# First MLP product in pairs of 512 and 256 columns, bias source in another buffer, another front and tail

## The chip, the cores and the metric
The kernel runs on one core of a Trainium2 chip. Its engines work side by side: TensorE (matmuls, in the profile PE), VectorE (DVE), ScalarE (ACT), GpSimd (POOL) and SyncE (SP), which mainly starts transfers; transfers run on DMA engines. Memory on the chip is SBUF (128 partitions) and PSUM, where matmuls write, in banks of 512 float columns. The metric is the device time of one execution in microseconds; smaller is better.

## The reference, cut to what matters
One layer of a hybrid decoder on 256 tokens of width 2048, in float32:
```
z = rmsnorm(h) @ w_in                      # q, k, v and two convolution parts u
h = h + concat(moba_attention(q, k, v, rel_bias), conformer_conv(u)) @ w_out
h = h + cross_attention(rmsnorm(h), rmsnorm(mem))      # wq, wk, wv, wo
h = h + square(relu(rmsnorm(h) @ w1)) @ w2             # w1: 2048 x 8192, w2: 8192 x 2048
return rmsnorm(h)
```
With 256 tokens and one block of 256, the block attention is causal attention with a bias that depends on the distance alone.

## The kernel before
All weights are cut on the host into 200 chunks of 128 x 2048 floats. One chunk is one *step*: 0 to 15 the convolution inputs, 16 to 23 the values, 24 to 39 queries and keys, 40 to 47 keys and values of the memory tokens, 48 to 63 the output projection, 64 to 71 the cross attention, 72 to 199 the MLP. The MLP runs four quarters of 32 steps: 16 steps of the first product, in four blocks of 512 hidden columns, then 16 of the second.

To keep float32 precision at TensorE's faster float32r form, each operand is split: ScalarE writes a rounded high part (`wh`, `actH`, `sH`), VectorE subtracts to get the low part (`wl`, `actL`, `sL`). A product is then three matmuls (`mm3`, line 104): high with high, high with low, low with high. In the first MLP product the weights are stationary (128 x 128) and 256 token columns of an activation part stream past; in the second the activations are stationary and 512 weight columns stream. So a step of the first product is 48 matmuls of 256 columns, one of the second 24 of 512.

A step's weights are loaded four steps ahead by SP into one of four buffers (`raw`) and split two steps ahead into one of three (`wh`, `wl`): the split for step j+2 waits until TensorE is through with step j-1. The loop at line 916 writes the order on every engine: for step j first the hooks "early", the load, the high split, the hooks "pre" (evacuations stand here), convolution taps on VectorE as filler, the low split, the hooks "late", the matmuls with "mid" hooks between them, and "post". Each engine works through its list in order.

Accumulation uses four PSUM banks in turn (`mm`): a block takes two. `evac_w1` (line 794) empties them by max with 0 and multiplying with the row norm `RB["2"]`, squares twice on ScalarE and subtracts on VectorE. For the first block the norm is not there in time, so it is emptied two steps later (`lag=2`, line 867), at step 78.

`ring` (line 91) is a set of seven buffers for short-lived tiles, taken in turn. The source of the attention bias, `rev` (line 261), is such a tile; ScalarE starts a transfer at step 8 that writes it 128 times to DRAM, and SP loads the bias back at step 20. The squares of the memory tokens for their norm (`Stats.add`, line 204) take ring tiles from step 8 on.

Where a tile stands in SBUF is set by `shifted` (line 176): with `ACT_SHIFT` the moving activation parts start 64 bytes past the weights modulo 512 bytes, in all products; with `S_SHIFT` the second product's stationary parts start at the same place modulo 512 as the weights that stream. In the value projections (steps 16 to 23 and 44 to 47) weights stream past activations, again 64 bytes apart.

At the end `finish` adds each token half's last bank to the sum, squares it on ScalarE with a row sum, takes the root, scales 2048 columns by halves on VectorE and ScalarE, and SP writes four pieces of 512 columns.

Of the kernel before, what the change touches and what calls it, by code (L numbers as in the profile page):

```python
# [9 lines left out]
F32 = mybir.dt.float32  # L10
F32R = mybir.dt.float32r
# [26 lines left out]
AHEAD = 2  # L38
WOUT_ORDER = [(0, 0), (1, 0), (2, 0), (0, 1), (1, 1), (2, 1), (3, 0), (3, 1)]
STEP_US = 5.25  # L40

ROOM = 128
ACT_SHIFT = {"H0": 16, "H1": 16, "H2": 112, "H3": 112, "L0": 16, "L1": 16, "L2": 112, "L3": 112}
S_SHIFT = {"Ha0": 32, "Ha1": 32, "Hc0": 96, "Hc1": 96, "La0": 32, "La1": 32, "Lc0": 96, "Lc1": 96}
MIX_STEP = 16

# [31 lines left out]
def tile_hybrid_block(ctx: ExitStack, tc: tile.TileContext, xT, memT, w, par, rel, gfin, out):  # L78
# [12 lines left out]
    def ring(shape=(P, 512)):  # L91
        return sb.tile(list(shape), F32, tag="ring", name=nm("ring"), bufs=7)
# [34 lines left out]
    nc.sync.dma_start(part[:, 0:CB], par[:, 0:CB])  # L127
    load(0)
    for i in range(4):
        nc.sync.dma_start(hT[0][:, i, :], xT[:, i, :])  # L130
        nc.sync.dma_start(raw[0][:, i * 512:(i + 1) * 512], w[0, :, i * 512:(i + 1) * 512])
    for g in range(1, 4):
        nc.sync.dma_start(hT[g], xT[:, 4 * g:4 * g + 4, :])
# [2 lines left out]
    relt = sb.tile([8, N_BUCKETS], F32, name="relt")  # L136
    nc.sync.dma_start(relt, rel)

    make_identity(nc, ident)
    pool.memset(ones, 1.0)  # L140


    hooks = {}
# [36 lines left out]
    def new_act(g):  # L180
        act_tiles[g] = tuple(shifted(f"act{x}{g}", ACT_SHIFT[f"{x}{g}"]) for x in "HL")

    def split_act(g, src, gain, i):
        hi, lo = act_tiles[g]
        c = col(gain, 4 * g + i)
        act.activation(hi[:, i, :], src[:, i, :], AF.Copy, scale=c)  # L186
        dve.scalar_tensor_tensor(lo[:, i, :], src[:, i, :], c, hi.bitcast(F32)[:, i, :],
                                 op0=OP.mult, op1=OP.subtract)

    def split_act_group(g, src, gain):  # L190
        new_act(g)
        for i in range(4):
            split_act(g, src, gain, i)

    def act_pair(kt):
        hi, lo = act_tiles[kt // 4]
        return hi[:, kt % 4, :], lo[:, kt % 4, :]


    class Stats:  # L200
# [57 lines left out]
    bias = sb.tile([P, 8, T], F32, tag="acc0", name="bias")  # L258

    def make_bias():  # L260
        rev = ring((8, 512))
        pool.memset(rev[:, 0:384], MASK)
        d = 0
        while d < T:
            e = d
            while e + 1 < T and bucket(e + 1) == bucket(d):
                e += 1
            b = bucket(d)
            pool.tensor_copy(rev[:, 255 - e:256 - d], relt[:, b:b + 1].to_broadcast([8, e - d + 1]))
            d = e + 1  # L270
        return rev
# [12 lines left out]
    def weight_stationary(j, banks, kg, acts, kts=4, cols=512, last=None):  # L284
# [9 lines left out]
            units.append(unit)  # L294
        return units

    def act_stationary(j, banks, kg, acts, last, ts=(0, 1), kts=4):
        units = []
        for i in range(kts):
            def unit(i=i):  # L300
                hi, lo = acts(kg * 4 + i)
                for t in ts:
                    s = slice(t * P, (t + 1) * P)
                    c = slice(i * 512, (i + 1) * 512)
                    mm3(banks[t], banks[t].ap, (hi[:, s], lo[:, s]), (wh[j][:, c], wl[j][:, c]),
                        last and i == kts - 1)
            units.append(unit)
        return units
# [17 lines left out]
    RB = {}  # L326

    def split_both(j, g):
        new_act(g)
# [464 lines left out]
    def evac_w1(b, banks):  # L794
        sT[b] = tuple(shifted(f"mix{x}{MIX[b]}", S_SHIFT[x + MIX[b]], f"s{x}{b}") for x in "HL")
        for n in range(2):
# [34 lines left out]
    def acc_square(t, cb):  # L831
        d = acc[t][:, cb * 512:(cb + 1) * 512]
        act.activation(ring(), d, AF.Square, accum_out=ssq[:, 8 * t + cb:8 * t + cb + 1])  # L833

    def finish(t, bk):
# [6 lines left out]
        for i in range(2):  # L842
            c = slice(1536 + i * T, 1536 + (i + 1) * T)
            d = acc[t][:, c]
            dve.tensor_tensor(d, bk.ap[:, i * T:(i + 1) * T], d, op=OP.add)
            act.activation(ring()[:, 0:T], d, AF.Square, accum_out=ssq[:, 8 * t + 3 + i:8 * t + 4 + i])
            pool.tensor_mul(d, d, gb[3][:, i * T:(i + 1) * T])
            dve.scalar_tensor_tensor(part_ if i == 0 else v, ssq[:, 8 * t + 3 + i:8 * t + 4 + i], 1.0 / D, part_,
                                     op0=OP.mult, op1=OP.add)
# [3 lines left out]
        dve.tensor_scalar(a, a, -0.5, 1.5, op0=OP.mult, op1=OP.add)  # L853
        dve.tensor_tensor(r, y, a, op=OP.mult)
        for c in (0, 1, 2, 3):
            d = acc[t][:, c * 512:(c + 1) * 512]
            if c in (1, 3):
                act.activation(d, d, AF.Copy, scale=r)
            else:
                dve.tensor_scalar(d, d, r, None, op0=OP.mult)  # L860
            nc.sync.dma_start(out[rows, c * 512:(c + 1) * 512], d)

    for q in range(4):
        j0 = MLP0 + 32 * q
        for b in range(4):
            block(j0 + 4 * b, 4, weight_stationary, act_pair, lambda bk, b=b: evac_w1(b, bk),
                  lag=2 if q == b == 0 else 0)
        for cb in range(4):
            jc = j0 + 16 + 4 * cb
            if q == 3 and cb == 3:  # L870
                banks = []

                def first(kg, jc=jc):
# [10 lines left out]
                pe_units[jc + 3] = lambda jc=jc: (  # L884
                    act_stationary(jc + 2, banks, 2, s_pair, False, ts=(1,))
                    + act_stationary(jc + 3, banks, 3, s_pair, True, ts=(1,)))
# [67 lines left out]
def weight_chunks(np, w_in, wk, wv, w_out, wq, wo, w1, w2):  # L954
    chunks = []

    def put(cols, rows):
        a = cols[rows]
        chunks.append(a.reshape(-1, P, a.shape[1]).transpose(1, 0, 2).reshape(P, 2048))
# [26 lines left out]
        put(wo[:, b * 512:(b + 1) * 512], slice(None))  # L986
    for q in range(4):
        for b in range(4):
            for g in range(4):
                put(w1[:, q * 2048 + b * 512:q * 2048 + (b + 1) * 512], rows(g))  # L990
# [41 lines left out]
```

## Time and profile before

| | us |
|---|---|
| median of 3 runs | 1175.96 |
| lowest, highest | 1175.51, 1176.62 |
| profiled execution, whole | 1174.24 |
| its span, first to last instruction | 1172.4 |
| PE busy | 1149.8 (98%) |
| DVE busy | 707.8 (60%) |
| ACT busy | 540.9 (46%) |
| POOL busy | 116.6 (10%) |

The profile is of one execution. Matmuls overlap each other in it, so a busy share of TensorE doesn't tell how fast they follow; that is read from a piece of the chain of waits, its time by its count. "x" is a count of instructions, "<-" names what an idle engine waited for, L a line of the kernel. Helpers hide the caller's line: all matmuls have line 101 and all VectorE work line 67, so operations are told apart by their tiles. "PEld" is a weight load, "SPq" and "ACTq" are starts of transfers. The granted clock is a share of TensorE's 2.4 GHz.

### The profile page before, as it was taken

To read this page: it belongs to the slowest core of one execution; us is meant where nothing else is said; L and a number is where in the kernel's file an instruction comes from. 1 tells how busy PE (TensorE), PEld (TensorE's weight loads), DVE (VectorE), ACT (ScalarE), POOL (GpSimd) and SP (SyncE) were. 2 spreads that over 40 slices of the span, in tenths; PEclk is the share of its full clock that TensorE was granted. 3 is DMA by queue.
4 is the path that set the end of the run, shared out by engine and by line. 5 is a ranking of instruction groups with operands and counts; after the bars stand their busy time and mean duration, and the time that the engine had idled before them with its cause. 6 is when DMAs were issued, how large, how long until landed. Compare 5 with 4: busy or idle time off the path is not lost.

```text
span 1172.4 us, 18441 instructions
## 1 busy us (share of the span) xinstructions
PE 1149.8 (98%) x7976; PEld 1073.0 (92%) x7976; DVE 707.8 (60%) x821; ACT 540.9 (46%) x564; POOL 116.6 (10%) x100
## 2 busy tenths in 40 slices
PE   7989999999999999999999999999999999999996
PEld 7988899999999999999889999889999888999885
DVE  6669998787666668555444545454555454445443
ACT  7525444565666456554333444333444333444342
POOL 2453121012003003000000000000000000000112
PEclk9998999999999999999999999999999999999998
DMA  8865654444554535545655544655554655554632
GB/s 340 288 186 180 221 204 169 162 147 177 184 193 168 199 120 180 216 145 192 240 195 200 180 180 175 221 182 199 193 181 150 227 198 182 190 195 153 217 142 72
DMA packets 35000, 221.02 MB, mean 189 GB/s; under 512 B 3816, under 2 KB 6504, under 8 KB 9448
## 3 DMA queue, kind: packets, MB, share of 16 engines
q1 hardware_dynamic: 33888, 218.29, 52.0%
q10 hardware_dynamic: 1032, 1.57, 0.9%
q8 instruction: 62, 1.02, 0.3%
q14 instruction: 18, 0.15, 0.0%
HBM read 216.18 MB, written 3.67 MB: 188 GB/s over the span
## 4 chain that ended last, share of the span: by engine, by line
PE 93%; DMA 4%; ACT 1%; DVE 1%; issue 0%; SPq 0%; ACTq 0%
PE mm L101 87%; PE cv L101 3%; DMA dram_rev<-ring 3%; PE sm L101 2%; DMA raw<-in_w_dram 1%; DVE wl L67 1%; ACT wh L160 0%; PE sm L813 0%; PE sm L499 0%; PE sm L689 0%; DVE small L67 0%; ACT actH L186 0%; ACT L679 0%; ACT ring L679 0%; ACT ring L210 0%
## 5 line engine op out<-in xcount | busy, mean ns | idle before, releaser
L67 DVE TENSOR_TENSOR wl<-raw,wh 128x2048 fp32r<-128x2048 f32 (+1 forms) x205 | 447.1, 2187 | 305.5 <-ACT wh L160 301.1
L160 ACT ACTIVATE wh<-raw 128x2048 fp32r<-128x2048 f32 x195 | 373.5, 1915 | 505.0 <-PE mm L101 462.5
L101 PE MATMUL mm<-actH,wh 128*128 128x256 f32 x1600 | 452.4, 283 | 11.0 <-ACT wh L334 6.3
L101 PE MATMUL mm<-actH,wl 128*128 128x256 f32 x1600 | 449.0, 281 | 1.8 <-DVE wl L67 1.8
L101 PE MATMUL mm<-actL,wh 128*128 128x256 f32 x1600 | 448.4, 280 | 0.0
L101 PEld LDWEIGHTS mm<-actH,wh 128*128 128x128 f32 x1600 | 302.9, 189 | 11.7 <-ACT wh L334 6.5
L101 PEld LDWEIGHTS mm<-actH,wl 128*128 128x128 f32 x1600 | 303.1, 189 | 2.5 <-DVE wl L67 2.5
L101 PEld LDWEIGHTS mm<-actL,wh 128*128 128x128 f32 x1600 | 302.4, 189 | 0.3
L101 PE MATMUL mm<-wh,sH 128*128 128x512 f32 x512 | 199.3, 389 | 0.0
L101 PE MATMUL mm<-wh,sL 128*128 128x512 f32 x512 | 199.2, 389 | 0.0
L101 PE MATMUL mm<-wl,sH 128*128 128x512 f32 x512 | 199.2, 389 | 0.0
L101 PEld LDWEIGHTS mm<-wh,sL 128*128 128x128 f32 x512 | 96.1, 188 | 20.2
L101 PEld LDWEIGHTS mm<-wl,sH 128*128 128x128 f32 x512 | 96.1, 188 | 19.8
L101 PEld LDWEIGHTS mm<-wh,sH 128*128 128x128 f32 x512 | 96.1, 188 | 19.7
L67 DVE SCALAR_TENSOR_TENSOR cv<-hp,part,cv 128x256 f32<-128x256 f32 x240 | 97.7, 478 | 0.0
L897 POOL TENSOR_TENSOR acc<-acc,gb 128x512 f32<-128x512 f32 x6 | 12.1, 2041 | 669.8 <-ACT ring L833 669.8
L67 DVE TENSOR_TENSOR sL<-ring,sH 128x512 fp32r<-128x512 f32 x32 | 22.2, 692 | 67.1 <-ACT sH L801 67.1
L211 POOL TENSOR_TENSOR acc<-acc,ring 128x512 f32<-128x512 f32 x17 | 35.7, 2098 | 163.4 <-ACT ring L210 162.7
L170 POOL TENSOR_TENSOR wl<-raw,wh 128x512 fp32r<-128x512 f32 x24 | 32.4, 1383 | 98.0 <-ACT wh L160 98.0
L101 PE MATMUL mm<-wh,actH 128*128 128x512 f32 x96 | 38.2, 398 | 0.0
L101 PE MATMUL mm<-wh,actL 128*128 128x512 f32 x96 | 37.9, 395 | 0.0
L101 PE MATMUL mm<-wl,actH 128*128 128x512 f32 x96 | 37.9, 395 | 0.0
(156 smaller groups left out, 1039.1 us busy)
## 6 DMA issues: line engine op xcount, KB each, us to landing
raw<-in_w_dram SPq DMA_DIRECT2D x199, 1024.0 KB, 4.8
mem<-in_memT_dram SPq DMA_DIRECT2D x4, 512.0 KB, 8.0
out_dram<-acc SPq DMA_DIRECT2D x8, 256.0 KB, 3.1
hT<-in_xT_dram SPq DMA_DIRECT2D x3, 512.0 KB, 8.2
dram_rev<-ring ACTq DMA_DIRECT2D x1, 1532.0 KB
raw<-in_w_dram SPq DMA_DIRECT2D x4, 256.0 KB, 4.4
bias<-dram_rev SPq DMA_DIRECT2D x1, 1024.0 KB, 9.1
gb<-in_gfin_dram SPq DMA_DIRECT2D x4, 256.0 KB, 7.0
```

Of the source, the lines that this page charges most:

```text
L67: return op(out, *args, **kw)
L101: pe.matmul(o, lhsT=lhsT, rhs=rhs, start=not bk.begun, stop=stop, skip_group_check=True)
L160: act.activation(wh[j], raw[j], AF.Copy)
L170: pool.tensor_sub(wl[j][:, s], raw[j][:, s], wh[j].bitcast(F32)[:, s])
L211: eng.tensor_tensor(self.acc, self.acc, sq, op=OP.add)
L897: pool.tensor_mul(d, d, gb[cb])
```

## The change
1. In the MLP the high and low part of an activation tile stand side by side in one tile, so one matmul streams both (512 columns) past a high weight part; one of 256 columns with the low weight part follows, added onto the high half's columns. A bank then holds 128 hidden columns: high-high plus low-high sums in its first half, the high-low sums in its second. Two banks take half a block (256 hidden columns) over two steps, and the weights are cut on the host to match. `evac_half` copies the second halves out by ScalarE, adds by VectorE and goes on as before. The first block of all keeps the old form.
2. In the MLP these tiles start at the same place modulo 512 bytes as the weights; before the MLP 64 bytes past, as they did.
3. `rev` takes a buffer of the convolution tiles (`hp`), which the fourth of these takes after it.
4. At the front the four small x loads go out on ScalarE's queue; a first small ScalarE instruction brings its function table load forward; 14 transposes of a constant run on TensorE.
5. At the end, the last half step fills its bank in two halves of 256 columns one after the other; `finish` adds and squares both before it folds them, one small operation is drawn into the final gain beforehand (`prepare_gain`), and the outputs leave in five pieces on two queues.

```diff
+WARM = 14
-ACT_SHIFT = {"H0": 16, "H1": 16, "H2": 112, "H3": 112, "L0": 16, "L1": 16, "L2": 112, "L3": 112}
+ACT_SHIFT = (0, 0, 96, 96)
...
-        nc.sync.dma_start(hT[0][:, i, :], xT[:, i, :])
+        act.dma_start(hT[0][:, i, :], xT[:, i, :])
...
+    act.activation(rr[:, 14:15], ones[:, 0:1], AF.Copy)
+    warm = bank("sm")
+    for i in range(WARM):
+        pe.transpose(warm.ap[:, (i % 4) * P:(i % 4 + 1) * P], ones, ident)
...
+    def new_act(g, gain):
+        t = sb.tile([P, 8 * T + ROOM], F32R, tag=f"act{g}", name=nm(f"act{g}"))
+        shift = (ACT_SHIFT[g] + (0 if gain == G_MLP else MIX_STEP)) % ROOM
+        act_tiles[g] = t[:, shift:shift + 8 * T].rearrange("p (a s b) -> p a s b", a=4, s=2)
...
-        rev = ring((8, 512))
+        rev = sb.tile([P, 2, T + CONV_K - 1], F32, tag="hp", name="rev", bufs=4)
+        rev = rev.rearrange("p a b -> p (a b)")[0:8, 0:512]
...
+    def paired(j, banks, g, last):
+        units = []
+        for u in range(4):
+            def unit(u=u):
+                for i in (2 * u, 2 * u + 1):
+                    kt = 8 * g + i
+                    both = act_tiles[kt // 4][:, kt % 4, :, :].rearrange("p s b -> p (s b)")
+                    for m in range(2):
+                        s = slice(i * 256 + m * P, i * 256 + (m + 1) * P)
+                        mm(banks[m], banks[m].ap, wh[j][:, s], both, False)
+                        mm(banks[m], banks[m].ap[:, 0:T], wl[j][:, s], both[:, 0:T], last and i == 7)
+            units.append(unit)
+        return units
...
+    def evac_half(b, half, banks):
+        if half == 0:
+            sT[b] = tuple(shifted(f"mix{x}{MIX[b]}", S_SHIFT[x + MIX[b]], f"s{x}{b}") for x in "HL")
+        y, s = ring((P, 2, T)), ring((P, 2, T))
+        d = slice(2 * half, 2 * half + 2)
+        for m in range(2):
+            act.copy(s[:, m, :], banks[m].ap[:, T:])
+            dve.tensor_tensor(y[:, m, :], banks[m].ap[:, 0:T], s[:, m, :], op=OP.add)
+        dve.scalar_tensor_tensor(y, y, 0.0, twice(RB["2"]), op0=OP.max, op1=OP.mult)
+        act.activation(s, y, AF.Square)
+        act.activation(sT[b][0][:, d, :], y, AF.Square)
+        dve.tensor_sub(sT[b][1][:, d, :], s, sT[b][0].bitcast(F32)[:, d, :])
+
+    def half_block(j0, b, half):
+        banks = []
+        def make(g):
+            if g == 0:
+                banks.extend([bank("mm"), bank("mm")])
+            return paired(j0 + g, banks, g, g == 1)
+        for g in range(2):
+            pe_units[j0 + g] = lambda g=g: make(g)
+        at("pre", j0 + 2, lambda: evac_half(b, half, banks))
...
-            block(j0 + 4 * b, 4, weight_stationary, act_pair, lambda bk, b=b: evac_w1(b, bk),
-                  lag=2 if q == b == 0 else 0)
+            if q == b == 0:
+                block(j0, 4, weight_stationary, act_pair, lambda bk: evac_w1(0, bk), lag=2)
+            else:
+                for half in range(2):
+                    half_block(j0 + 4 * b + 2 * half, b, half)
...
+    def last_units(jc, banks):
+        units = []
+        for half in range(2):
+            o = banks[1].ap[:, half * T:(half + 1) * T]
+            for kg in (2, 3):
+                def unit(half=half, kg=kg, o=o):
+                    for i in range(4):
+                        hi, lo = s_pair(kg * 4 + i)
+                        c = slice(i * 512 + half * T, i * 512 + (half + 1) * T)
+                        mm3(banks[1], o, (hi[:, P:], lo[:, P:]), (wh[jc + kg][:, c], wl[jc + kg][:, c]),
+                            kg == 3 and i == 3)
+                units.append(unit)
+        return units
```

How instructions move. TensorE, at the border of steps 77 and 78 (`wh77`, `wh78` are weights of the step; `mm_` a bank's tile), before:

```order
L101 MATMUL mm_253_5100<-actH1_236_4817,wh77_5040 128x256
L101 MATMUL mm_253_5100<-actL1_237_4818,wh77_5040 128x256
L101 MATMUL mm_253_5100<-actH1_236_4817,wl77_5041 128x256
L101 MATMUL mm_252_5099<-actH2_242_4890,wh78_5095 128x256
L101 MATMUL mm_252_5099<-actL2_243_4891,wh78_5095 128x256
L101 MATMUL mm_252_5099<-actH2_242_4890,wl78_5096 128x256
```

After:

```order
L102 MATMUL mm_236_5099<-act3_233_4969,wh77_5040 128x512
L102 MATMUL mm_236_5099<-act3_233_4969,wl77_5041 128x256
L102 MATMUL mm_237_5100<-act3_233_4969,wh77_5040 128x512
L102 MATMUL mm_237_5100<-act3_233_4969,wl77_5041 128x256
L102 MATMUL mm_252_5219<-act0_220_4727,wh78_5095 128x512
L102 MATMUL mm_252_5219<-act0_220_4727,wl78_5096 128x256
L102 MATMUL mm_253_5220<-act0_220_4727,wh78_5095 128x512
L102 MATMUL mm_253_5220<-act0_220_4727,wl78_5096 128x256
```

Before, step 78 adds to the banks that step 77 filled; after, it opens two new ones (`mm_252`, `mm_253`), the buffers that the first block's tiles `mm_226` and `mm_227` had.

VectorE, the evacuation of the first block at step 78 (`sL0` is the low part of its result), before:

```order
L67 SCALAR_TENSOR_TENSOR ring_260_5226<-mm_240_4838,Rb_257_5181 128x512
L67 TENSOR_TENSOR sL0_259_5225<-ring_261_5227,sH0_258_5224 128x512
L67 SCALAR_TENSOR_TENSOR ring_262_5232<-mm_241_4839,Rb_257_5181 128x512
L67 TENSOR_TENSOR sL0_259_5225<-ring_263_5233,sH0_258_5224 128x512
L67 TENSOR_TENSOR wl80_5222<-raw80_5093,wh80_5221 128x2048
```

After:

```order
L68 SCALAR_TENSOR_TENSOR ring_244_5194<-mm_226_4840,Rb_241_5161 128x512
L68 TENSOR_TENSOR sL0_243_5193<-ring_245_5195,sH0_242_5192 128x512
L68 SCALAR_TENSOR_TENSOR ring_246_5200<-mm_227_4841,Rb_241_5161 128x512
L68 TENSOR_TENSOR sL0_243_5193<-ring_247_5201,sH0_242_5192 128x512
L68 TENSOR_TENSOR ring_250_5208<-mm_236_5099,ring_251_5209 128x256
L68 TENSOR_TENSOR ring_250_5208<-mm_237_5100,ring_251_5209 128x256
L68 SCALAR_TENSOR_TENSOR ring_250_5208<-ring_250_5208,Rb_241_5161 128x512
L68 TENSOR_TENSOR sL1_249_5207<-ring_251_5209,sH1_248_5206 128x512
L68 TENSOR_TENSOR wl80_5190<-raw80_5093,wh80_5189 128x2048
```

Between the first block's evacuation and the low split for step 80 now stands that of the first half block (`mm_236`, `mm_237`).

SP, the first transfers of the program, before:

```order
L127 DMA part_67<-in_par_dram 128x64
L130 DMA hT0_69<-in_xT_dram 128x256
L131 DMA raw0_74<-in_w_dram 128x512
L130 DMA hT0_69<-in_xT_dram 128x256
L131 DMA raw0_74<-in_w_dram 128x512
L130 DMA hT0_69<-in_xT_dram 128x256
L131 DMA raw0_74<-in_w_dram 128x512
L130 DMA hT0_69<-in_xT_dram 128x256
L131 DMA raw0_74<-in_w_dram 128x512
L133 DMA hT1_70<-in_xT_dram 128x1024
L125 DMA raw1_84<-in_w_dram 128x2048
```

After, on SP and then on ScalarE:

```order
L128 DMA part_67<-in_par_dram 128x64
L132 DMA raw0_74<-in_w_dram 128x512 x4
L134 DMA hT1_70<-in_xT_dram 128x1024
L126 DMA raw1_84<-in_w_dram 128x2048
L134 DMA hT2_71<-in_xT_dram 128x1024
```

```order
L131 DMA hT0_69<-in_xT_dram 128x256 x4
L143 ACT_TABLE_LOAD
L143 ACTIVATE rr_68<-ones_66 128x1
L194 ACTIVATE act0_2_118<-hT0_69,part_67 128x256
L359 ACTIVATE wh0_119<-raw0_74 128x512
```

The x loads (`hT0`) have left the list in front of `raw1` and stand ahead of ScalarE's first work.

## Rows read from the trace of the kernel before

**Rows 1.** The page: span, TensorE busy, TensorE busy and granted clock by slice.
```profile
span 1172.4 us, 18441 instructions
...
PE 1149.8 (98%) x7976; PEld 1073.0 (92%) x7976; DVE 707.8 (60%) x821; ACT 540.9 (46%) x564; POOL 116.6 (10%) x100
...
PE   7989999999999999999999999999999999999996
...
PEclk9998999999999999999999999999999999999998
```

**Rows 2.** Chain that ended last: start us, us, what; 50 to 103.
```profile
50.25 36.14 DMA dram_rev<-ring
...
88.87 2.30 DVE wl L67
...
91.21 11.24 PE mm L101 x70
```

**Rows 3.** Timeline of PE, 82 to 92: start us, us, instruction, wait before it.
```profile
83.96 0.28 PE L101 MATMUL mm<-actH,wl 128*128 128x256 f32 x1
88.89 0.58 PE L101 MATMUL mm<-actH,wh 128*128 128x256 f32 x1 [4.65 <-ACT wh L160]
...
91.21 0.58 PE L101 MATMUL mm<-actH,wl 128*128 128x256 f32 x1 [1.53 <-DVE wl L67]
```

**Rows 4.** Timeline of ScalarE, 50 to 100.
```profile
86.41 0.63 ACT L210 ACTIVATE ring<-mem 128x512 f32<-128x512 f32 x1 [16.77 <-DMA dram_rev<-ring]
```

**Rows 5.** Busy us by engine (x instructions), PE clock, DMA share, GB/s; one stretch.
```profile
80.00:100.00 20.00, 13.82 (x89) 13.32 (x89) 11.13 (x17) 8.31 (x9) 8.96 (x7) 0.74 0.39 141
```

**Rows 6.** Chain in stretches of one shape: MLP products, value projection, then MLP front.
```profile
649.89 60.18 PE mm L101 x511
...
559.95 60.07 PE mm L101 x265
...
119.89 30.33 PE mm L101 x130
...
443.98 29.92 PE mm L101 x264
```

**Rows 7.** Timeline of VectorE, 464 to 500.
```profile
481.30 0.68 DVE L67 SCALAR_TENSOR_TENSOR ring<-mm,Rb 128x512 f32<-128x512 f32 x1
486.00 0.69 DVE L67 TENSOR_TENSOR sL<-ring,sH 128x512 fp32r<-128x512 f32 x1 [4.02 <-ACT sH L801]
486.61 0.68 DVE L67 SCALAR_TENSOR_TENSOR ring<-mm,Rb 128x512 f32<-128x512 f32 x1
...
489.18 4.48 DVE L67 TENSOR_TENSOR wl<-raw,wh 128x2048 fp32r<-128x2048 f32 x2
```

**Rows 8.** Timeline of ScalarE, 464 to 500.
```profile
478.96 0.35 ACT L245 COPY Rb<-sm 128x256 f32<-128x256 f32 x1
483.01 1.91 ACT L160 ACTIVATE wh<-raw 128x2048 fp32r<-128x2048 f32 x1 [3.70 <-issue]
484.83 0.61 ACT L800 ACTIVATE ring<-ring 128x512 f32<-128x512 f32 x1
485.35 0.62 ACT L801 ACTIVATE sH<-ring 128x512 fp32r<-128x512 f32 x1
```

**Rows 9.** Chain that ended last, front.
```profile
5.61 8.64 DMA raw<-in_w_dram
...
14.94 0.70 DVE wl L67
...
15.69 26.89 PE mm L101 x226
```

**Rows 10.** Timeline of VectorE, 1150 to 1173.
```profile
1162.85 0.42 DVE L67 TENSOR_TENSOR acc<-mm,acc 128x256 f32<-128x256 f32 x1 [0.90 <-PE mm L101]
...
1163.93 0.42 DVE L67 TENSOR_TENSOR acc<-mm,acc 128x256 f32<-128x256 f32 x1
...
1165.99 0.16 DVE L67 TENSOR_TENSOR rr<-small 128x1 f32<-128x1 f32 x1
```

More of the change, by code (lines that the diff above doesn't have):

```diff
@@ L137, in tile_hybrid_block @@
     nc.sync.dma_start(relt, rel)
+    pool.memset(ones, 1.0)
     make_identity(nc, ident)
-    pool.memset(ones, 1.0)
+    act.activation(rr[:, 14:15], ones[:, 0:1], AF.Copy)
+    warm = bank("sm")
+    for i in range(WARM):
+        pe.transpose(warm.ap[:, (i % 4) * P:(i % 4 + 1) * P], ones, ident)
     hooks = {}
@@ L178, in shifted @@
         return t[:, shift:shift + 4 * T].rearrange("p (a b) -> p a b", a=4)
-    def new_act(g):
-        act_tiles[g] = tuple(shifted(f"act{x}{g}", ACT_SHIFT[f"{x}{g}"]) for x in "HL")
+    def new_act(g, gain):
+        t = sb.tile([P, 8 * T + ROOM], F32R, tag=f"act{g}", name=nm(f"act{g}"))
+        shift = (ACT_SHIFT[g] + (0 if gain == G_MLP else MIX_STEP)) % ROOM
+        act_tiles[g] = t[:, shift:shift + 8 * T].rearrange("p (a s b) -> p a s b", a=4, s=2)
     def split_act(g, src, gain, i):
-        hi, lo = act_tiles[g]
+        hi, lo = act_tiles[g][:, i, 0, :], act_tiles[g][:, i, 1, :]
         c = col(gain, 4 * g + i)
-        act.activation(hi[:, i, :], src[:, i, :], AF.Copy, scale=c)
-        dve.scalar_tensor_tensor(lo[:, i, :], src[:, i, :], c, hi.bitcast(F32)[:, i, :],
-                                 op0=OP.mult, op1=OP.subtract)
+        act.activation(hi, src[:, i, :], AF.Copy, scale=c)
+        dve.scalar_tensor_tensor(lo, src[:, i, :], c, hi.bitcast(F32), op0=OP.mult, op1=OP.subtract)
     def split_act_group(g, src, gain):
-        new_act(g)
+        new_act(g, gain)
         for i in range(4):
@@ L195, in act_pair @@
     def act_pair(kt):
-        hi, lo = act_tiles[kt // 4]
-        return hi[:, kt % 4, :], lo[:, kt % 4, :]
+        t = act_tiles[kt // 4]
+        return t[:, kt % 4, 0, :], t[:, kt % 4, 1, :]
     class Stats:
@@ L328, in split_both @@
     def split_both(j, g):
-        new_act(g)
+        new_act(g, G_MIX)
         split_tiles(j)
@@ L833, in acc_square, with prepare_gain @@
         act.activation(ring(), d, AF.Square, accum_out=ssq[:, 8 * t + cb:8 * t + cb + 1])
+    def prepare_gain():
+        for g in gb:
+            pool.tensor_scalar(g, g, -0.5, None, op0=OP.mult)
+    at("late", MLP0 + 24, prepare_gain)
     def finish(t, bk):
@@ L841, in finish @@
         dve.tensor_scalar(part_, v, 1.0 / D, EPS, op0=OP.mult, op1=OP.add)
-        for i in range(2):
-            c = slice(1536 + i * T, 1536 + (i + 1) * T)
-            d = acc[t][:, c]
+        ends = [acc[t][:, 1536 + i * T:1536 + (i + 1) * T] for i in range(2)]
+        for i, d in enumerate(ends):
             dve.tensor_tensor(d, bk.ap[:, i * T:(i + 1) * T], d, op=OP.add)
+        for i, d in enumerate(ends):
             act.activation(ring()[:, 0:T], d, AF.Square, accum_out=ssq[:, 8 * t + 3 + i:8 * t + 4 + i])
             pool.tensor_mul(d, d, gb[3][:, i * T:(i + 1) * T])
+        for i in range(2):
             dve.scalar_tensor_tensor(part_ if i == 0 else v, ssq[:, 8 * t + 3 + i:8 * t + 4 + i], 1.0 / D, part_,
@@ L852, in finish @@
         dve.scalar_tensor_tensor(a, v, y, y, op0=OP.mult, op1=OP.mult)
[L853 to L857, printed above, removed]
+        dve.scalar_tensor_tensor(r, a, -3.0, y, op0=OP.add, op1=OP.mult)
+        for lo, hi, on_act in ((0, 256, False), (1280, 1664, True), (256, 768, False), (1664, 2048, True),
+                               (768, 1280, False)):
+            d = acc[t][:, lo:hi]
+            if on_act:
                 act.activation(d, d, AF.Copy, scale=r)
+                act.dma_start(out[rows, lo:hi], d)
             else:
                 dve.tensor_scalar(d, d, r, None, op0=OP.mult)
-            nc.sync.dma_start(out[rows, c * 512:(c + 1) * 512], d)
+                nc.sync.dma_start(out[rows, lo:hi], d)
+    def last_units(jc, banks):
[11 more added lines that the diff above has]
+        return units
     for q in range(4):
@@ L883, in tile_hybrid_block @@
                     + act_stationary(jc + 3, banks, 3, s_pair, True, ts=(0,)))
-                pe_units[jc + 3] = lambda jc=jc: (
-                    act_stationary(jc + 2, banks, 2, s_pair, False, ts=(1,))
-                    + act_stationary(jc + 3, banks, 3, s_pair, True, ts=(1,)))
+                pe_units[jc + 3] = lambda jc=jc: last_units(jc, banks)
                 at("pre", jc + 3, lambda: finish(0, banks[0]))
@@ L988, in weight_chunks @@
         for b in range(4):
+            c = w1[:, q * 2048 + b * 512:q * 2048 + (b + 1) * 512]
             for g in range(4):
-                put(w1[:, q * 2048 + b * 512:q * 2048 + (b + 1) * 512], rows(g))
+                if q == b == 0:
+                    put(c, rows(g))
+                else:
+                    put(c[:, (g // 2) * 256:(g // 2 + 1) * 256], slice((g % 2) * 1024, (g % 2 + 1) * 1024))
         for cb in range(4):
```

## The prediction, made before the changed kernel ran

> **What bounds the kernel now.** I read the page's busy shares and slices first. TensorE is busy 98% of the span; its busy share dips in the first, the third and the last slice, its clock in the fourth and the last [rows 1]. So time can only come from four places: the rate at which matmuls follow each other, the dip between 59 and 117 us (third and fourth slice), the front and the tail. The chain of waits, read next, gives each.
>
> *The dip.* The chain leaves TensorE at 50.25 and runs 36.14 us through the transfer that spreads the bias source to DRAM, then through a weight split to TensorE at 91.21 [rows 2]. ScalarE's timeline names the link: a squaring for the memory tokens sat 16.77 us until that transfer, which reads a ring buffer, ended [rows 4]; the next weight split stood behind it. TensorE's last matmul before it starts at 83.96, two more run at 88.89 and the next at 91.21 [rows 3], and the clock is only 0.74 in that stretch [rows 5].
>
> *The rate.* Busy times overlap on this engine, so I divide pieces of the chain by their counts [rows 6]. First MLP product: 60.18/511 = 117.8 ns for 256 columns. Second product, 512 columns: 60.07/265 = 226.7. The value projection, also 512: 30.33/130 = 233.3. End of the cross attention and first steps of the MLP, again 256 columns: 29.92/264 = 113.3. So either shape has two rates, 3 to 4% apart. What differs between the two 512-column stretches is the place: by the program's addresses the moving and the stationary tile start at the same place modulo 512 bytes in the second MLP product, and 64 bytes apart in the value projection. The 256-column products are all 64 bytes apart, and show both rates.
>
> **The change, part by part**, against the profiled execution (1174.24 us, 1172.4 us of it span; the median of the runs shown is 1.7 above it).
>
> *Bias source off the ring.* The transfer stays, its source moves to a buffer that the fourth convolution tile takes over, written at step 16, which begins near 101 (16 steps of 5.65 us behind a front of some 10), after the transfer's 86.4. What goes: the gap 84.08 to 88.89, 4.81 us; from 88.89 to 91.21 two matmuls' worth of work, 2.32 - 0.24 = 2.08; and 70 matmuls in 11.24 us [rows 2] where 70 x 0.1178 = 8.25 do, 2.99, the price of the half clock. Sum -9.8. What is late next there is nothing that the trace shows: VectorE is free until the split, and the steps before ran at 5.65 us. Range -9 to -9.9.
>
> *Pairs.* 60 of the 64 steps of the first product change, 16 pairs each: 960. Three matmuls of 117.8 are 353.3 ns. A pair is one of 512 and one of 256 columns, the 512 like the second product (same place): 226.7. No row shows 256 columns at the same place; it lies between 113.3 and 117.8. I take 113.3, half of 226.7, since the 512 at that place shows no extra over that ratio: 340.0, a gain of 13.3 ns, 960 x 13.3 = -12.8 us. Bounds: 233.3 + 117.8 = 351.1 gains 2.2 ns, -2.1 us. On the other side, the slow-clock matmuls at 91.21 and after come 213 ns apart; at twice the clock that is 106.7 per 256 columns, 320 a pair, -32. I stay by the nearer row.
> The first block (4 steps) and the last half step keep or get 256 columns at the same place: 240 matmuls now at 113.3 that may become 117.8, 0 to +1.1; I take +0.3.
>
> The Trainium skill (TensorE: Matmul & The Clock Gate, Part 2, step ①) says that the array reads SBUF through two independent ports, so that loading the next weights takes nothing from the running matmul; and Part 1 (Wait — 56ns) puts a fixed 2.5 ns on each matmul. By that, place would not matter and a pair would save 2.5 ns, 2.4 us in all, and the sum would be 1163.7. The two 512-column rates (226.7 and 233.3) disagree with the first sentence.
>
> *The added evacuation work.* Each half block adds two ScalarE copies (0.35 each by [rows 8]) and two VectorE adds (0.42, [rows 10]) per two steps. The chain of one half block: split 1.9, two copies 0.7, last add 0.42, max-multiply 0.68, squares 0.61 and 0.62, subtract 0.69, low split 2.24 [rows 7, 8]: 7.9 us, some 8.2 with the gaps. It must end before the second next step, 2 x 5.44 = 10.9 us. Hidden, cost 0; 2.7 us of slack.
>
> *A wait the change adds.* The first block still waits two steps for its gain and is evacuated at step 78. Four banks go round. Before, the next block held the other two until step 80. Now half a block is done after two steps, and step 78 opens the first block's two banks while they are still full. TensorE's second pair at step 78 must wait for the second max-multiply of that evacuation, which stands on VectorE behind a subtract that waits for ScalarE, itself behind the split for step 80. In the trace of before that split starts at 483.01, as step 78 does, and the second max-multiply runs from 486.61 to 487.29 [rows 7, 8]: 4.4 us into the step. TensorE has 0.34 us of work there: it idles about 4.05 us, and all behind it on TensorE waits too. Cost +4.05 (3.5 to 4.4). Step 80's own weights are then not late: its low split ends some 12.1 us after step 78 began, its need comes after 15.9.
>
> *Front.* The four small x loads leave SP for ScalarE's queue, so the load that ends the front's chain, issued at 5.61 and followed by a split and TensorE at 15.69 [rows 9], is issued 4 x 0.47 = 1.9 us earlier. It landed after 8.64 us among transfers that share the engines, so not all of that comes back: 0 to -1.9, I take -1.3. The 14 transposes and the early table load run while TensorE and ScalarE wait for data; the warmer clock is hidden behind this load.
>
> *Tail.* With the last bank in two halves, the first add, square and fold run beside the second half's matmuls: one round, 1163.93 - 1162.85 = 1.08 us [rows 10], and one small VectorE step less, 0.18. Outputs on two queues start some 0.15 us sooner; the same bytes leave. -1.4 (-0.8 to -1.8). The factor that goes into the final gain is multiplied in on GpSimd at step 96; nothing asks for the gain before the last quarter, so it costs 0.
>
> Sum: -9.8 - 12.8 + 0.3 + 4.05 - 1.3 - 1.4 = -20.95, so 1174.24 - 20.95 = 1153.3. The runs lie up to 2.4 above the profiled execution; the dip and the front, where the clock's state can differ between executions, are mostly gone, so I add less than half of the 1.7: **1154**.
>
> **Rivals.**
> 1. *The clock falls at step 78.* For: at the dip the clock was down after a gap of 4.81 us [rows 3, 5]. Against: 4.05 is shorter, and work resumes without a second wait. Price by the dip: up to 2.99 us, and it may be partly hidden: 1156 to 1157.
> 2. *Place is not what made 226.7*, or the 256-column half does not profit: the pair costs 351.1 or between. -2.1 in place of -12.8: up to 1164.5. For: nothing shows 256 columns at one place. Against: two stretches of the same shape that differ in place.
> 3. *Pairs are better than the rows*, toward 320: 1153 down to 1135. Against: no full-clock row at that rate; with a part of it, 1147.
> 4. *Slower.* The evacuation decides: if the chain of a half block, 8.2 us by rows, stretches beyond 10.9 us, each us over costs TensorE 1 us at 30 half blocks. From 11.6 us on it eats the whole gain; at 12.4 us, 30 x 1.5 = 45 us, 1199. For: ScalarE and VectorE hand over four times in it. Against: 2.7 us of slack, and of 10.9 us VectorE is busy 6.7 (two low splits and the four steps above), ScalarE 5.8.
> That the change does not do what it says can be excluded for the ring and for the pairs; for the front it is the lower bound 0.
>
> **How the numbers follow.** Forecast 0.52 (own range 1151 to 1157); rival 1: 0.20; rival 2: 0.17; rival 3: 0.07; rival 4: 0.04. Within 0.2%, 2.35 us, is about what a measurement of this kernel can't tell from no change; only rival 4 near its threshold ends there. Faster 0.95, same 0.015, slower 0.035. The range 1148 to 1164 takes in rivals 1 and 2 and the better part of the unknown rate, and leaves rival 4 and the far end of 3 out.
>
> **What would show it.** No ScalarE wait for the bias transfer, and clock 1.00 near 85 us: ring right. First-product steps of 5.44 us, with pairs 340 ns apart: rate right; 5.62 would be rival 2. One TensorE gap of about 4 us near 455 to 460, ended by VectorE, with or without slow matmuls behind it. TensorE's steady stream from about 14.4 in place of 15.69. About 1.2 us from the last matmul's add to the scale less than the 3.3 of before. Wrong: any gap at each second step of the first product, or a second gap near 85.

## The result and the profile after

| | before | after |
|---|---|---|
| median, us | 1176.29 (4 runs) | 1168.99 (4 runs) |
| lowest, highest | 1175.51, 1178.01 | 1168.52, 1169.38 |
| span of the profiled execution | 1172.4 | 1166.9 |

The ratio is 0.9936, 95% interval 0.9919 to 0.9953: 7.3 us faster, where 22 were forecast. 1169.0 lies above the range of 1148 to 1164. Faster was right; the size was not. The profiled executions differ by 5.6 us (1174.24 to 1168.66), their spans by 5.5; no trace here shows the rest of the 7.3.

The page of after, against [rows 1]: span, TensorE, its busy share and its clock by slice.

```profile
span 1166.9 us, 16727 instructions
...
PE 1151.2 (99%) x7054; PEld 1030.3 (88%) x7054; DVE 730.2 (63%) x881; ACT 558.0 (48%) x625; POOL 123.2 (11%) x104
...
PE   8999999999999999899999999999999999999997
...
PEclk9999999999999999999999999999999999999999
```

The dip of the third and fourth slice is gone. But TensorE is still busy for 1151 us, about as before (1149.8): where the matmuls were to become faster, busy time did not fall. A smaller dip is new in slice 17.

The chain of after: front, the stretch of the old ring stall, the first block of the MLP, and a stretch of pairs.

```profile
5.47 7.52 DMA raw<-in_w_dram
...
14.43 15.58 PE mm L102 x130
...
59.89 31.56 PE mm L102 x268
...
439.96 20.04 PE mm L102 x167
...
649.88 50.18 PE mm L102 x284
```

Front: the steady stream begins at 14.43 instead of 15.69 [rows 9]. Ring: 268 matmuls follow each other without a break through the place where before stood still [rows 2, 3], at 31.56/268 = 117.8 ns. First block: 20.04/167 = 120.0 ns, slower than the 113.3 of [rows 6]. Pairs: 50.18/142 = 353.4 ns, exactly three matmuls of 117.8. The pairs gained nothing.

Stretches of after, columns as in [rows 5]: the old stall, and step 78.

```profile
80.00:100.00 20.00, 20.00 (x170) 19.81 (x169) 19.59 (x38) 8.74 (x8) 6.38 (x6) 1.00 0.71 250
...
473.00:485.00 12.00, 7.95 (x40) 6.74 (x39) 6.23 (x8) 6.60 (x11) 0.00 (x0) 0.86 0.21 82
```

The timeline of TensorE around that second stretch (start us, us, instruction, wait before it):

```profile
473.21 0.27 PE L102 MATMUL mm<-act,wl 128*128 128x256 f32 x1
477.53 0.77 PE L102 MATMUL mm<-act,wh 128*128 128x512 f32 x1 [4.05 <-DVE ring L68]
478.10 0.42 PE L102 MATMUL mm<-act,wl 128*128 128x256 f32 x1
478.31 0.63 PE L102 MATMUL mm<-act,wh 128*128 128x512 f32 x1
...
478.95 0.63 PE L102 MATMUL mm<-act,wh 128*128 128x512 f32 x1
...
479.60 0.63 PE L102 MATMUL mm<-act,wh 128*128 128x512 f32 x1
...
480.73 0.40 PE L102 MATMUL mm<-act,wh 128*128 128x512 f32 x1
```

and of VectorE, to set beside [rows 7]:

```profile
471.78 0.68 DVE L68 SCALAR_TENSOR_TENSOR ring<-mm,Rb 128x512 f32<-128x512 f32 x1
476.10 0.69 DVE L68 TENSOR_TENSOR sL<-ring,sH 128x512 fp32r<-128x512 f32 x1 [3.63 <-ACT sH L826]
476.70 0.68 DVE L68 SCALAR_TENSOR_TENSOR ring<-mm,Rb 128x512 f32<-128x512 f32 x1
```

One gap of 4.05 us, ended by the second max-multiply behind the subtract: the wait that the prediction described. Behind it the clock was at half: five pairs took 480.73 - 477.53 = 3.20 us, where 5 x 0.353 = 1.77 do. Rival 1 came true, for 1.4 us in this execution.

The tail, VectorE of after, to set beside [rows 10]: the last two adds, the factor, the first scale.

```profile
1158.50 0.76 DVE L68 TENSOR_TENSOR acc<-mm,acc 128x256 f32<-128x256 f32 x2 [1.49 <-PE mm L102]
...
1161.00 0.16 DVE L68 SCALAR_TENSOR_TENSOR rr<-small 128x1 f32<-128x1 f32 x1
1161.20 1.15 DVE L68 TENSOR_SCALAR acc<-acc,rr 128x256 f32<-128x256 f32 x3
```

From the first of the adds that follow the last matmul to the factor it takes 2.50 us, before 3.14; from that add to the end of the span 8.4, before 9.6.

By the starts of the steps in both traces, the span's -5.5 us is: ring -9.6, front -1.3, tail -1.2; against it step 78 +5.6, first block +1.3, last half step +0.3; pairs 0.0. The other -0.6 is spread over steps 30 to 71 and steps 76 to 87.

### The profile page after: what moved, and what is told of

Same layout as the page of the kernel before. It is cut to its first block, busy times and chain, and to the rows that moved or that the text cites. A ratio compares the mean times of both kernels' runs of the same rounds, so it can differ in the third digit from the quotient of the medians.

```text
span 1166.9 us, 16727 instructions
## 1 busy us (share of the span) xinstructions
PE 1151.2 (99%) x7054; PEld 1030.3 (88%) x7054; DVE 730.2 (63%) x881; ACT 558.0 (48%) x625; POOL 123.2 (11%) x104
## 4 chain that ended last, share of the span: by engine, by line
PE 96%; ACT 1%; DMA 1%; DVE 1%; issue 1%; ACTq 0%
PE mm L102 90%; PE cv L102 3%; PE sm L102 2%; DMA raw<-in_w_dram 1%; DVE wl L68 0%; DMA hT<-in_xT_dram 0%; ACT wh L166 0%; PE sm L862 0%; PE sm L524 0%; PE sm L714 0%; DVE small L68 0%; ACT act L194 0%; ACT L704 0%; ACT acc L914 0%; ACT ring L704 0%
## 5 line engine op out<-in xcount | busy, mean ns | idle before, releaser
L102 PE MATMUL mm<-act,wh 128*128 128x256 f32 (+1 forms) x2240 | 570.4, 332 | 5.4 <-DVE ring L68 4.0
L102 PE MATMUL mm<-act,wl 128*128 128x256 f32 x1600 | 449.3, 281 | 0.2 <-DVE wl L68 0.2
L102 PEld LDWEIGHTS mm<-act,wh 128*128 128x128 f32 x2240 | 377.8, 189 | 50.9 <-issue 4.3
L102 PEld LDWEIGHTS mm<-act,wl 128*128 128x128 f32 x1600 | 303.1, 189 | 0.8 <-DVE wl L68 0.7
L102 PE MATMUL mm<-wh,sH 128*128 128x512 f32 (+1 forms) x520 | 200.6, 386 | 0.0
L102 PE MATMUL mm<-wl,sH 128*128 128x512 f32 (+1 forms) x520 | 200.6, 386 | 0.0
L102 PE MATMUL mm<-wh,sL 128*128 128x512 f32 (+1 forms) x520 | 200.6, 386 | 0.0
L102 PE MATMUL mm<-wh,act 128*128 128x512 f32 x192 | 61.3, 397 | 0.0
L102 PEld LDWEIGHTS mm<-wh,act 128*128 128x128 f32 x192 | 36.1, 188 | 8.5
L102 PE MATMUL mm<-wl,act 128*128 128x512 f32 x96 | 38.0, 395 | 0.0
```

The costliest lines, as they stand in the source:

```text
L102: pe.matmul(o, lhsT=lhsT, rhs=rhs, start=not bk.begun, stop=stop, skip_group_check=True)
```

## The experiments

The question is the pairs: why did 512 columns that start at the weights' place modulo 512 not run at 226.7 ns?

**Two scans of the common place.** Only the start of the MLP's activation tiles changes, a different one for each of the four tiles.

```diff
-        shift = (ACT_SHIFT[g] + (0 if gain == G_MLP else MIX_STEP)) % ROOM
+        shift = (ACT_SHIFT[g] + ((0, 16, 32, 48)[g] if gain == G_MLP else MIX_STEP)) % ROOM   # first scan
+        shift = (ACT_SHIFT[g] + ((64, 80, 96, 112)[g] if gain == G_MLP else MIX_STEP)) % ROOM # second scan
```

> In the MLP the four activation tiles start 0, 64, 128 and 192 bytes past the weights' place modulo 512, so each step of pairs shows two places and the first block's four steps show one place each for matmuls of 256 columns. The changed kernel has pairs of 353.3 ns on the mean (241+120, 236+113, 233+117 in turn) and 256-column matmuls of 120.0 in its first block, all at place 0. Theory P (the place sets the pair's time): tile 0 stays near 353, another tile comes to 340 to 347 per pair; the first block's second step (64 bytes) is 113 to 118 per matmul. Rival L (a long and a short matmul in turn cost 353 wherever they stand): all four tiles within 2 ns of 353. Time of the whole under P 1162 to 1172, as some places may be worse; under L 1168 to 1169.

> As the run before with places 256, 320, 384 and 448 bytes. Theory P: at least one tile clearly off 353 per pair; the value projection (64 bytes the other way, 448) has 233.3 per 512 columns, so the last tile should not be below 346. Rival L: all within 2 ns of 353.

Measured 1167.5 and 1169.3 (before 1173.7 beside them); 1.2 us of the difference is step 78, with a longer half clock. TensorE in the first scan, the first matmul of the second tile in a step, and eight pairs later the first of the next step:

```profile
650.51 0.39 PE L102 MATMUL mm<-act,wh 128*128 128x512 f32 x1
...
653.34 0.40 PE L102 MATMUL mm<-act,wh 128*128 128x512 f32 x1
```

That is 2.83 us for eight pairs. Reckoned so from the unrounded starts, in the steps after the first quarter, a pair takes 351.7, 353.1, 350.7 and 352.8 ns on the four tiles of the first scan, and the same within 0.1 ns in the second. The first block's four steps, one place each, take 119.9, 117.9, 118.6 and 114.0 ns per 256 columns, again alike in both. So the place repeats every 256 bytes, not 512, and none of the four common places makes a pair fast: theory P as stated failed, and rival L is nearly right. Places matter for 256 columns all the same.

**Each matmul's place against the weights loaded during it.** While a matmul streams, the weights of the next are loaded. The timeline of after shows it (PEld is a weight load): low weights (`wl`) are loaded from the start of the 512 columns, the next high ones (`wh`) from that of the 256.

```profile
660.79 0.40 PE L102 MATMUL mm<-act,wh 128*128 128x512 f32 x1
660.79 0.19 PEld L102 LDWEIGHTS mm<-act,wl 128*128 128x128 f32 x1
661.02 0.28 PE L102 MATMUL mm<-act,wl 128*128 128x256 f32 x1
661.02 0.19 PEld L102 LDWEIGHTS mm<-act,wh 128*128 128x128 f32 x1
```

Here the activations stand 64 bytes past the high weights, and in the paired steps the low weights are moved by the same 64 bytes. So the 512 stand at 0 against what is loaded during them, as in the second product, and the 256 at 64, as in the block that ran at 113.3.

```diff
+        o = 16 if j >= MLP0 + 4 and (j - MLP0) % 32 < 16 else 0   # floats
+        wl[j] = t[:, o:o + 2048]
...
-        shift = (ACT_SHIFT[g] + (0 if gain == G_MLP else MIX_STEP)) % ROOM
+        shift = (ACT_SHIFT[g] + MIX_STEP) % ROOM
```

> The weights that are loaded while a matmul streams are those of the next one: low parts during the 512 columns, high parts during the 256. Here the activations start 64 bytes past the high parts and the low parts are moved by 64 bytes in the paired steps, so the streaming 512 and the low weights share a place, and the streaming 256 and the high weights lie 64 bytes apart. Theory P in this sharper form (each matmul's time is set by its place against the weights loaded during it): 226.7 + 113.3 to 117.8 = 340 to 344.5 per pair, 960 pairs 8.5 to 12.8 us less, and the first block at 113 to 118 instead of 120 (0.4 to 1.3 less): 1155 to 1160. Rival L: 353 per pair, 1167.5 to 1168.5.

Measured 1155.4. The chain between 650 and 700, this kernel:

```profile
649.93 50.09 PE mm L103 x295
```

50.09/147.5 = 339.6 ns a pair; by the starts eight pairs apart it is 340.0 on all four tiles. The second tile of the first scan has its activations and high weights at the same places and differs in the low weights' place; its pairs took 353.1. So moving the low weights by 64 bytes is worth 13 ns a pair.

A rival is that a matmul's own weights decide, not those loaded meanwhile. In a pair both readings use the same two distances with the roles changed over: here the 512 stand 64 bytes from their own weights and the 256 at 0. The sums tell them apart. By own weights this pair would be 233.3 + 120.0 = 353.3, by the weights loaded meanwhile 226.7 + 113.3 = 340.0. The second is what was measured.

**The order in a pair group.** Both 512s, then both 256s, at the change's own places.

```diff
+                    for m in range(2):
                         mm(banks[m], banks[m].ap, wh[j][:, cs[m]], both, False)
+                    for m in range(2):
                         mm(banks[m], banks[m].ap[:, 0:T], wl[j][:, cs[m]], both[:, 0:T], last and i == 7)
```

> The changed kernel with the four matmuls of a row of the weights in another order: both of 512 columns first, then both of 256, so lengths change half as often. Rival L: half of the 6.7 ns that 353.3 has over 226.7 + 120.0 goes, 350 per pair, 3 us in all: 1165.5 to 1166. Theory P: still 353 or, by other phases, 346.7 to 354: 1162.5 to 1169.

Measured 1164.7; the chain from 650 to 700:

```profile
649.88 50.16 PE mm L102 x288
```

50.16/144 = 348.3 ns, within theory P's bounds and under rival L's 350. All places are 0 here as in after, and 5 of its 353.4 ns are regained by order alone: a matmul's rate depends on its neighbours too, not only on its own place.

**All sixteen combinations.** Activation tile g stands 64 x g bytes past the high weights, and the low weights move by 64 x q bytes in quarter q.

```diff
+        o = 16 * ((j - MLP0) // 32) if j >= MLP0 and (j - MLP0) % 32 < 16 else 0
...
+        shift = (ACT_SHIFT[g] + (16 * g if gain == G_MLP else MIX_STEP)) % ROOM
```

> Pairs, activation tile g at 64 x g bytes past the high weights, low weights moved by 64 x q bytes in quarter q: 16 combinations of the place of the 512 columns (against the low weights loaded during them, 64 x (g - q)) and of the 256 columns (against the next high weights, 64 x g). Theory: only where the 512 stand at 0 and the 256 at 64 (tile 1 of quarter 1) is a pair 340 ns; all others 345 to 356, the mirrored one (512 at 64, 256 at 0) 233.3 + 120.0 = 353. Rival: it is enough that the two places differ: all four tiles of quarter 1 near 340. Total 1166 to 1169.

Measured 1163.4. Timeline of TensorE: first matmul of tile 1 in quarter 1 (512 at 0, 256 at 64) and the one eight pairs later; then the mirrored places (64 and 0), tile 0 in quarter 3.

```profile
659.98 0.39 PE L103 MATMUL mm<-act,wh 128*128 128x512 f32 x1
...
662.71 0.40 PE L103 MATMUL mm<-act,wh 128*128 128x512 f32 x1
...
1009.85 0.40 PE L103 MATMUL mm<-act,wh 128*128 128x512 f32 x1
...
1012.65 0.40 PE L103 MATMUL mm<-act,wh 128*128 128x512 f32 x1
```

2.73/8 = 341 ns against 2.80/8 = 350. The rest by the same reckoning, ns a pair in the last steps of each quarter:

```
low weights moved by     tile 0    tile 1    tile 2    tile 3
  0 bytes                 351.9     353.1     350.6     352.8
 64                       346.6     341.9     347.4     350.8
128                       349.7     347.6     351.1     350.1
192                       351.1     348.0     346.4     349.5
```

One of sixteen reaches 342, the one expected, though not the 340.0 of the run where all four tiles stand so. In one run, then, the same tile goes from 353.1 to 341.9 when the low weights alone move by 64 bytes. The rival is out: the other tiles of that quarter take 346.6 to 350.6. The mirrored places, which by a matmul's own weights would be the 340 ns, take 350 to 351. Elsewhere, that the two places differ is worth a few ns (346 to 351; where they are alike, 351 to 353). The whole was under the range forecast for it (1166 to 1169).

**Are the pairs needed at all?** First they are undone: the old three matmuls of 256 columns, activations 64 bytes past the weights as before; ring, front and tail stay.

```diff
-            if q == b == 0:
-                block(j0, 4, weight_stationary, act_pair, lambda bk: evac_w1(0, bk), lag=2)
-            else:
-                for half in range(2):
-                    half_block(j0 + 4 * b + 2 * half, b, half)
+            block(j0 + 4 * b, 4, weight_stationary, act_pair, lambda bk, b=b: evac_w1(b, bk),
+                  lag=2 if q == b == 0 else 0)
```

> The pairs alone are undone: all 64 first-product steps of the MLP in the old form, three matmuls of 256 columns, activations 64 bytes past the weights as before; ring, front and tail stay changed. Theory: at a common place a pair costs what three matmuls cost (353 ns by the runs so far), so nothing is lost in the rate, and the step-78 wait with its slow clock (5.6 us) and the slower first block (1.3 us) go: about 1160.5 where before takes 1173.65. Rival: the pairs did win something that the last traces hide: 1166 or more.

Measured 1163.2, one run; 2.7 more than expected and 5.8 under after. Of the 2.7 about 1 us lies ahead of the MLP (it starts at 439.17, in after at 438.12). From there to the start of the last half step it takes 707.9 us, in after 714.4: 6.5 less, close to the 6.9 worked out. The change as made was better without its pairs.

Then the same scan of sixteen places with three matmuls:

> The old form (three matmuls of 256 columns) with activation tile g at 64 x g bytes past the high weights, and the low weights moved by 64 x q bytes in quarter q: 16 combinations, one step each per block. Theory (a matmul's spacing follows its place against the weights loaded during it, and 256 columns have two rates at 64): tile 1 of quarter 0 runs at 113.3 or 117.8 (5.44 or 5.65 us a step), tile 0 of quarter 0 at 120.0 (5.76); somewhere a combination may hold 113.3 in all its steps. If one does, the pairs were not needed for the 340.0 ns. Rival: no combination of three 256s stays below 115; then the 512-column matmul is needed to get there. Total 1158 to 1165.

Measured 1164.7. The chain in two steps of quarter 2, where the low weights are moved by 128 bytes (steps 142 and 143, tiles 2 and 3):

```profile
833.38 5.70 PE mm L103 x48
...
839.09 5.33 PE mm L103 x47
```

Tile 3, at 192 bytes, runs at 5.33/47 = 113.4 ns, and comes back to it in every block of that quarter from neighbours at 118.8. In the last three quarters all others settle between 116 and 120; in the first, 64 and 0 bytes gave the 117.9 and 119.9 expected. Tile 1 in this quarter ran one step at 113.3 and then steps at 118.9: some places have two rates and hold one of them for a whole step or longer. This scan does not separate the two readings, since three matmuls have the same three distances by either.

**The step-78 wait.** Placed pairs, and both max-multiplies of the first block ahead of the squares and the subtract:

```diff
+        ys = [ring((P, 2, T)) for _ in range(2)]
         for n in range(2):
-            y, s = ring((P, 2, T)), ring((P, 2, T))
+            dve.scalar_tensor_tensor(ys[n], pair(banks[n].ap), 0.0, twice(RB["2"]), op0=OP.max, op1=OP.mult)
+        for n in range(2):
+            y, s = ys[n], ring((P, 2, T))
```

> Placed pairs (the run at 1155.4), and in the first block's evacuation both max-multiplies stand ahead of the squares and the subtract on VectorE. Theory: both banks are read by the time step 78 begins, the gap of 4.3 us and the slow clock behind it (1.5 us) go: 1149.6 (1149 to 1151.5). Rival: another wait stands behind it (the weight split for step 80, delayed as before): only 1 to 3 us go, 1152.5 to 1154.5.

Measured 1150.1, 5.3 less than with the wait; step 78 takes 6.04 us, 11.81 with it. VectorE in step 77, and the stretch with the clock:

```profile
470.52 1.28 DVE L69 SCALAR_TENSOR_TENSOR ring<-mm,Rb 128x512 f32<-128x512 f32 x2
```

```profile
473.00:485.00 12.00, 12.00 (x74) 10.64 (x73) 7.84 (x8) 8.46 (x13) 0.00 (x0) 1.00 0.30 107
```

Both banks are read by 471.8, TensorE has no gap and the clock stays at 1.00. No second wait stood behind it, as the theory had it.

**Three versions side by side.** The first is the kernel before with other places and nothing else: activations 192 bytes past the high weights, low weights moved by 128, and both weight parts at the activations' place in the value projections.

```diff
-ACT_SHIFT = {"H0": 16, "H1": 16, "H2": 112, "H3": 112, "L0": 16, "L1": 16, "L2": 112, "L3": 112}
+ACT_SHIFT = {"H0": 48, "H1": 48, "H2": 16, "H3": 16, "L0": 48, "L1": 48, "L2": 16, "L3": 16}
-MIX_STEP = 16
+MIX_STEP = 48
+        if 16 <= j < 24 or 44 <= j < 48:
+            oh = ol = MIX_STEP
+        elif j < MLP0 or (j - MLP0) % 32 < 16:
+            oh, ol = 0, 32
+        else:
+            oh = ol = 0
```

> The kernel before with nothing but other places: activations 192 bytes past the high weights, low weights moved by 128 bytes (the combination of the scan that held 113.4 ns in its steps), and in the value projections both weight parts at the place of the activations. No pairs, no other ring, front or tail. Theory (place against the weights loaded meanwhile sets the rate, the form does not): 60 steps of the MLP and some 45 before it go from 117.8 to 113.4 ns, 0.21 us a step, and 12 value steps from 5.60 to 5.44: -22.5 - 1.9, about 1149 where before takes 1173. Rival: 113.4 held only because the neighbouring steps stood elsewhere; then steps fall back to 117.8 to 118.9 and the time is 1171 to 1177.

> The changed kernel with the pairs undone (the run at 1163.2) and the same places. Theory: 1163.2 - 12.8 (MLP) - 9.5 (before it) - 1.9 (values) = 1139. Rival as for the kernel before: no gain, 1161 to 1167.

> Placed pairs without the step-78 wait (the run at 1150.1), and the same places as the other two in all steps ahead of the MLP. Theory: 1150.1 - 9.5 - 1.9 = 1138.7, within 0.2% of the version without pairs, since a pair and three matmuls then take 340 ns alike. Rival: the pairs are worth something of their own and this one is 3 us or more ahead of the one without.

| kernel | median, us | ratio to before (1174.66) |
|---|---|---|
| before, places alone | 1153.09 | 0.9811 [0.9795, 0.9826] |
| after without pairs, places | 1142.16 | 0.9723 [0.9703, 0.9743] |
| after with pairs, places, no wait at 78 | 1141.82 | 0.9727 [0.9707, 0.9746] |

The chain from 650 on in each of the three:

```profile
649.96 40.12 PE mm L102 x354
```

```profile
649.99 40.12 PE mm L103 x354
```

```profile
649.97 40.12 PE mm L103 x236
```

40.12/354 = 113.3 ns, three of which are 340.0; 40.12/118 = 340.0 ns a pair. The two forms tie, in rate and in time. The value projection of the first version, with both places at 0 where they were 64 bytes apart [rows 6]:

```profile
119.99 12.01 PE mm L102 x53
```

12.01/53 = 226.6 ns instead of 233.3: there the place was the whole difference. Places alone take 21.6 us off the kernel before, three times what the whole change did. They missed 1149 by 4: the ring stall ends when its transfer ends, so 2.3 us of what the faster steps ahead of it win are lost in it again (step 14 starts 0.5 us earlier, not 2.8). The other two missed 1139 by 3. In the version without pairs 1.7 of it is a new wait in step 14, where the timeline of TensorE shows:

```profile
88.59 0.28 PE L103 MATMUL mm<-act,wl 128*128 128x256 f32 x1
90.75 0.61 PE L103 MATMUL sm<-ones,acc 128*128 128x1 f32 x4 [1.89 <-DVE acc L69]
```

VectorE is late there once TensorE is faster. In the version with pairs step 14 is 0.8 us longer than in the run at 1150.1, and the first block runs at 117.8 ns where that run had 113.3 at the same places, 0.9 us: two rates again, now between two kernels. The cause of the rest stays open.

## Why the prediction was wrong

*Ring*, -9.8 (its three terms add up to 9.88): measured -9.6 by the steps, no wait and full clock in [rows 2 to 5]'s stretch. Right. *Front*, -1.3: right, 15.69 to 14.43 [rows 9]. *Tail*, -1.4: -1.2 after allowing for the slower last half step; the way from add to factor shrank by 0.6, not 1.2; the other 0.6 lies behind the factor, in scales and outputs. That the sum came out near is in part luck: its pieces did not.

*Pairs*, -12.8: the step that failed; measured 0.0. The term took a pair as the sum of two rates from stretches of one shape each, 226.7 + 113.3 = 340.0, and 13.4 ns were missing.

Half of them is the 256 columns. "No row shows 256 columns at the same place; it lies between 113.3 and 117.8" was a bound without a row. The first block of after is that row, 120.0, outside the bound and 6.7 over what I took. The other half is the adding up: 226.7 + 120.0 = 346.7, measured 353.4. Beside those 256s the 512s do not run at 226.7, and with the order alone changed the pair takes 348.3. Rival 2 (chance 0.17) was the case, with its price: even its 351.1 was too good by 2.3 ns.

"What differs between the two 512-column stretches is the place" was right: the value projection, moved to one place, runs at 226.6. But I compared where a matmul's own two operands start. In the second product and in the value projection a matmul's own weights and those loaded during it stand alike, so [rows 6] could not tell the two distances apart. In the pairs of after both are 0, so this mistake alone doesn't explain their 353.4; it is why I took this place for a fast one. Measured against the weights loaded meanwhile, places that differ, 0 for the 512 and 64 bytes for the 256, gave the 340.0; my reading, with the 120.0 since measured, would have put them at 353.3.

And the 113.3 in [rows 6] was one of two rates at the same place, as the 117.8 in the same rows says; I saw that "the 256-column products are all 64 bytes apart, and show both rates" and did not draw the conclusion that the theory of place, as I had it, lacked something.

*First block and last half step*, +0.3: +1.3 and +0.3, by the same 120.0 ns.

*Step 78*, +4.05: right in its mechanism, read from [rows 7, 8]; the idle time is 4.05, and that the hundredth agrees is luck. The place, "near 455 to 460", was a slip: step 78 began at 482.9, and the prediction's own ring and front terms put it at 471.8; the gap begins at 473.5. The clock behind it (rival 1, chance 0.20) added 1.4. I had argued that 4.05 us is shorter than the 4.81 of [rows 3]; but no row showed a gap near 4 us that left the clock up, so the argument had nothing under it.

*Evacuation hidden*: right, no gap at the second steps of after, and rival 4 did not come. The forecast stayed 15 us under the result: pairs +12.8, the step's clock and the first block most of the rest.

The Trainium skill (TensorE: Matmul & The Clock Gate, Part 2, step ①) says that the stream and the weight load have a read port each and that the load takes no read bandwidth from the running matmul. Here moving the low weights by 64 bytes changed a pair from 353.1 to 340.0 ns, so for these float32r products the spacing does depend on where the weights stand; by what mechanism no run shows. The fixed 2.5 ns on each matmul that the Trainium skill states (TensorE: Matmul & The Clock Gate, Part 1, Wait — 56ns) do not show as a saving either: the best pair and the best three matmuls take 340.0 both.

What stays open: why these places are fast, why some keep either of two rates, and why the 512 of after run at 233 to 241 beside slow 256s although their place, by either measure, is that of the second product. No run here separates a matmul's place from the state its neighbour leaves.

## What to carry to other kernels

When two stretches of one shape run at different rates, list everything that differs between them, the operands of the next instruction included, and move one address at a time; a scan over four buffers and four loop stages gave sixteen combinations in one run. Two rates at the same settings mean that a variable is missing, and a gain should not be priced at the better of the two. Rates of two shapes, each taken from a stretch of its own, need not add up when the shapes take turns. Before a rewrite is judged, undo its form and keep its side effects: here the form was worth nothing, and the places alone 21.6 us.

## What the runs showed of the hardware

At full clock (2.4 GHz) the best steady spacings are 113.3 ns = 272 cycles for 256 columns and 226.7 ns = 544 for 512, 16 more than one per column for each 256 columns; the slow steady ones are 117.8, 118.8 and 120.0 ns (283, 285 and 288 cycles). At the places tried, steps of 64 bytes, the place counts modulo 256 bytes.

At half clock (1.2 GHz) no cost of the place shows. In after, two pairs behind the gap at step 78 take 479.60 - 478.31 = 1.29 us, 0.64 each; 768 columns at one cycle each would be 640 ns. In the run at 1155.4, with the low weights moved, a pair takes the same 0.64 there, and in before 256 columns take 213 ns behind the stall, again one cycle each. At full clock these three take 353.4, 340.0 and 117.8.

Around the end of the gap of 4.05 us the clock fell to half, for 3.4 us; in the second scan, after the same kind of gap, for 6.8. The gap of 1.89 us in step 14 of the version without pairs was not followed by a fall, its stretch:

```profile
85.00:97.00 12.00, 10.11 (x89) 9.92 (x88) 11.63 (x25) 4.07 (x4) 0.78 (x2) 1.00 0.58 212
```

The clock is 1.00 throughout, and VectorE is busy for 11.63 of the 12 us: TensorE's one wait in it is for VectorE.
